# Attention scores: the low part of the queries against the first 1024 keys, in two halves of the array

## The chip, the cores and the metric

The kernel runs on one NeuronCore of a Trainium2 chip. The metric is the device time of one execution in microseconds (us). Three runs of the kernel before gave 2132.44, 2133.23 and 2136.51 us, so the median is 2133.23 us.

## The reference

One layer of a diffusion backbone over 1024 latent tokens of width 1024, with 256 context tokens as a prefix. Only the attention branch matters here: eight heads, each with two softmax maps of width 64, over 1280 keys (1024 latent, 256 context). Cut to what is computed:

```
z = modulate(x, norm1_w, sh1, sc1) @ w_in
q, k = rms_norm(...), rms_norm(...)            # per head and map, width 64, then rotary
s = einsum('bqhmd,bkhmd->bhmqk', q, k_all) * 64 ** -0.5
p = softmax(s, axis=-1)
a = p[:, :, 0] - lam * p[:, :, 1]              # difference of the two maps
o = einsum('bhqk,bkhe->bqhe', a, v_all)
...                                            # S5 branch, gated merge, w_out
x = x + ga1 * merge_branches(...)
x = x + ga2 * conv_ffn(modulate(x, norm2_w, sh2, sc2), w_up, conv_w, conv_b, w_down)
```

All arrays are float32.

## The kernel before

The kernel has three phases. Phase A normalises the tokens, projects them, prepares the S5 branch and spills queries, keys, values and gates to DRAM. Phase B is the attention. Phase C merges the branches and runs the feed-forward part.

Precision: a float32 operand is kept as two float32r parts, a high part and the rest (the low part). `Qd` and `Kd` hold both parts (index `i`). For a head and a map, the tile `K` (L1213) has the high part of the keys on partitions 0 to 63 and the low part on partitions 64 to 127, for 1280 keys. A tile `q` (L1225) holds one part of the queries, and the same 64 rows stand on both halves of the partitions. So one product of 128 rows of a `q` tile with `K` gives that part of the queries times both parts of the keys.

Phase B works on pairs of token tiles, 32 pairs in all (four pairs to a head), in a loop whose order on TensorE, VectorE and ScalarE is written out by hand (`manual_schedule`). In a pair there are four score tiles: two token tiles (`a`, `b`) by two maps, each 128 tokens by 1280 keys in three banks of PSUM (tile `sc`, two of them in flight). `attn_scores` (L1232 to L1241) makes a score tile from six products: for the columns 0 to 512, 512 to 1024 and 1024 to 1280, the high part of the queries (`Q[0]`, L1238) and then the low part (`Q[1]`, L1239). Then VectorE takes the row maximum (L1240), ScalarE the exponentials (L993), VectorE combines the two maps (L1011), TensorE transposes the result (L1020), ScalarE copies the transposes out of PSUM into `at` tiles (L1027, nine buffers), and TensorE multiplies them with the values (L1038). The four score tiles of a pair stand between transposes and value products of the pairs before, so that what follows a score tile on TensorE is a value product (L1038) for two of the four and a transpose (L1020) for the other two.

The loads of phase B are issued by SyncE (SP), whose order a scheduler sets: `K` (L1214), values `V` (L1217), and `q` (L1227 and L1228, eight transfers for half a head). SP issues in order, so a load that waits for a buffer holds back those behind it. Four `K` buffers and four `q` buffers let a head's keys, and half a head's queries, be loaded ahead.

At the start of phase B, TensorE also has four blocks of the S5 branch's last projection to do (`fill`, L1265 to L1267 on tiles `ta` and `tb`), between the first score tiles.

Two other helpers use part of the array and serve the prediction. `ada_part` (L302) multiplies four times with 32 columns of weights, at a place of the array given by `tile_position`. L896 transposes blocks of 32 rows. Both stand between products that use the whole array, such as L417 to L419, L554 to L556 and L891.

Of the kernel before, what the change touches and what calls it, by code (L numbers as in the profile page):

```python
# [10 lines left out]
F32R = mybir.dt.float32r  # L11
# [7 lines left out]
P = 128  # L19
D = 1024          # model width  # L20
KT = D // P       # feature tiles of the model width
L = 1024          # latent tokens
NT = L // P       # token tiles; token n = NT * p + t
NC = 256          # context tokens
LK = L + NC
NKT = LK // P
H = 8             # heads
HD = 64           # width of one map of a head
G = 32            # S5 groups
GC = 16           # channels of a group  # L30
NS = 64           # states of a group
# [7 lines left out]
CH = 8            # tokens per S5 chunk  # L39
NCH = L // CH     # latent chunks  # L40
NCC = NC // CH    # context chunks
FF_PARTS = (5, 5, 4, 4, 4)

# columns of the packed per-partition parameters
# [7 lines left out]
# columns of the constants  # L52
# [4 lines left out]
def pack(x, c, ctx, c_ctx, ada_w, ada_b, norm1_w, w_in, b_gate, q_norm_w, k_norm_w,  # L57
# [3 lines left out]
    """Data layout only: every array sent is a rearrangement of the inputs or depends on shapes alone."""  # L61
    A = {}

    def put(name, a):
        A[name] = np.ascontiguousarray(a)
# [3 lines left out]
    c2 = np.stack([np.asarray(c)[0], np.asarray(c_ctx)], 0)                 # [2, D]  # L69
    put("c2", c2.reshape(2, KT, P).transpose(2, 1, 0))                      # [P, KT, 2]  # L70
    aw = np.asarray(ada_w)[0]
    put("ada0", aw[:, :2048].reshape(KT, P, 2, 4, 256).transpose(3, 1, 0, 2, 4))            # [4, P, KT, 2, 256]
    put("ada", aw[:, 2048:].reshape(KT, P, 2, 4, 512).transpose(2, 0, 1, 3, 4))

    # inside a head map: (row/col, half, i) -> (half, row/col, i)
    def perm64(a):
# [7 lines left out]
    put("win", np.stack([s.reshape(2, 4, P, 512).transpose(0, 2, 1, 3) for s in slabs]))   # [11, 2, P, 4, 512]  # L84
    put("rows", np.concatenate([perm64(np.asarray(q_norm_w)), perm64(np.asarray(k_norm_w)), np.asarray(lam_q1),
                                np.asarray(lam_k1), np.asarray(lam_q2), np.asarray(lam_k2)], 1))  # [1, 384]
# [3 lines left out]

    def st(a):                                                              # [2, G, NS] -> [(d p), G]
        return np.asarray(a).transpose(0, 2, 1).reshape(P, G)

# [15 lines left out]
    def wtiles(a):                                                          # [K, M] -> [M/P, P, K/P, P]  # L109
        k, m = a.shape  # L110
        return a.reshape(k // P, P, m // P, P).transpose(2, 1, 0, 3)
# [8 lines left out]
    # constants of the shapes  # L120
# [3 lines left out]
    n = (NT * np.arange(P)[:, None] + np.arange(NT)[None, :])               # [P, NT]  # L124
# [3 lines left out]
    cs, sn = np.cos(ang), np.sin(ang)                                       # [P, NT, 2, 16]  # L128
# [6 lines left out]
def r32(ap):  # L135
    return ap.bitcast(F32)


class Kern:
# [24 lines left out]
    def pst(self, shape):  # L164
        """One of two banks of PSUM, in turn."""
        self.turn = 1 - self.turn
        return self.t(self.psT, shape, ("ta", "tb")[self.turn], 1)

# [1 line left out]
    def rsqrt_act(self, pool, v, r, tmp):  # L170
        """r = v ** -0.5: seed from the tables, one Newton step."""
# [7 lines left out]
    def rsqrt_dve(self, pool, v, n, tag, bufs=2):  # L179
        """v ** -0.5 on VectorE: seed from the bits, three Newton steps."""  # L180
# [73 lines left out]
    # ---------------------------------------------------------------- phase A  # L254
    def ada_load(self, pool, qt):
        """Weights of shift and scale of the first norm for a quarter of the features."""
# [6 lines left out]
    def ada_first(self, ps, crep, aw):  # L263
        """Two partial sums over the rows of the weights."""
# [27 lines left out]
    def ada_part(self, pool, ps, crep, grp):  # L292
        """Modulation vectors of a group of columns, streamed; yields after each part of the weights."""
# [24 lines left out]
    def phase_a(self):  # L318
# [15 lines left out]
        p0, p0_st = self.pool("p0", "right")  # L334
        TA = 5                                              # token tiles of the first part
# [6 lines left out]
        def pieces(part, k):  # L342
            """Parts of the activations, columns of the input, row of the modulation."""
# [24 lines left out]
        def norm1(acc, late):  # L368
            """Mean square of each token, its -1/2 power on the diagonal of a block, in two parts."""
# [21 lines left out]
        def spread(d):  # L391
            """The scale of each token on all partitions."""
# [8 lines left out]
        def modulate(part, rb, ks):  # L401
            """x s1 rb + shift, as two float32r parts."""
# [197 lines left out]
    def rope_tables(self, zp, kind):  # L600
        """cos and sin times the norm's weights, for queries with the scale of the scores."""
# [18 lines left out]
    def lam(self, zp):  # L620
# [7 lines left out]
        # minus lambda  # L628
# [4 lines left out]
    def qk_post(self, zp, ps, pz, kind, hs, tt):  # L633
        """RMS norm over each head map, rotary, then transposed to [map and width, token]."""
# [68 lines left out]
    def sincos_dve(self, zp, x, n):  # L703
# [20 lines left out]
        # quadrant: k mod 4 = 2 b + o  # L724
# [3 lines left out]
        stt(f, f, -4.0, k, op0=OP.mult, op1=OP.add)             # k mod 4  # L728
# [4 lines left out]
        ts(sb, b, -2.0, 1.0, op0=OP.mult, op1=OP.add)           # sign of the sine  # L733
        ts(cb, o, -2.0, 1.0, op0=OP.mult, op1=OP.add)
        tt(cb, cb, sb, op=OP.mult)                              # sign of the cosine
        ts(d, o, -1.0, 1.0, op0=OP.mult, op1=OP.add)            # 1 - o
# [11 lines left out]
    def cmul(self, eng, o, a, b, tmp):  # L748
        """o = a b on pairs (re, im)."""
# [779 lines left out]
```

## Time and profile before

| | |
|---|---|
| Median of three runs | 2133.23 us (2132.44 to 2136.51) |
| Profiled execution, its span | 2136.6 us |
| TensorE (PE) busy | 2063.8 us, 97% of the span |
| PE weight loads (PEld) busy | 1702.4 us, 80% |
| VectorE (DVE) busy | 1190.6 us, 56% |
| ScalarE (ACT) busy | 743.6 us, 35% |
| GpSimd (POOL) busy | 814.7 us, 38% |
| Phase B, first to last score product | 828.1 to 1202.8 us of the span |

The profiled execution reads like the slowest of the three: its span is within 0.1 us of the highest run and 3.4 us (0.16%) above the median. The ends of matrix products are modelled and overlap, so the busy time of PE is no measure of speed; the distance between the starts of two successive products is what the engine takes for one. A row of PEld is the load of the stationary operand of a product. The granted clock of TensorE is a column of the views by stretch.

### The profile page before, as it was taken

The page shows a single profiled execution, that of the slowest core. Times are in us where ns is not written, and L with a number is a line of the kernel's source. Part 1 is how long each engine was busy: PE and PEld are TensorE (multiplying, and loading weights), DVE is VectorE, ACT ScalarE, POOL GpSimd, SP SyncE. Part 2 cuts the span into 40 slices and gives each one's busy share as a digit, 9 for nine tenths or more (in the row PEclk, how much of TensorE's full clock was granted, in tenths as well). Part 3 has the DMA queues.
Part 4 walks back from the last instruction along what each step waited for, and adds up shares of the span by engine and source line. Part 5 has one row for each costly group of instructions (what it writes and reads, how often), then busy time and mean ns, then how long its engine had stood idle before and what let it go on. Part 6 is the DMA issues. An engine that isn't in the chain of part 4 may idle for free. (4 is left out here: it accounts for less than half of the span.)

```text
span 2136.6 us, 28496 instructions
## 1 busy us (share of the span) xinstructions
PE 2063.8 (97%) x10656; PEld 1702.4 (80%) x10656; DVE 1190.6 (56%) x2363; ACT 743.6 (35%) x1349; POOL 814.7 (38%) x923
## 2 busy tenths in 40 slices
PE   6998999998899999999999989999999999999998
PEld 4777778866577887999999878878888888888887
DVE  6998944799972133888888653443323322233233
ACT  4443424221222312788878601322212212112121
POOL 1476411234311531366666645433323323233221
PEclk9999999999999999999999999999999999999999
DMA  9345565345666327322331145111111111111102
GB/s 323 112 108 139 125 189 176 111 136 165 187 203 220 117 99 227 111 77 77 107 92 53 36 146 185 60 45 50 47 52 50 46 43 45 45 55 43 52 15 99
DMA packets 150506, 227.84 MB, mean 107 GB/s; under 512 B 27104, under 2 KB 85856, under 8 KB 150368
## 3 DMA queue, kind: packets, MB, share of 16 engines
q1 hardware_dynamic: 140288, 207.67, 32.4%
q10 hardware_dynamic: 10080, 18.35, 2.3%
q8 instruction: 84, 1.38, 0.3%
q14 instruction: 54, 0.44, 0.1%
HBM read 168.76 MB, written 57.21 MB: 106 GB/s over the span
## 5 line engine op out<-in xcount | busy, mean ns | idle before, releaser
L1266 PE MATMUL up<-act,whi 128*128 128x512 f32 x704 | 277.3, 394 | 2.4 <-POOL act L1419 2.1
L1265 PE MATMUL up<-act,whi 128*128 128x512 f32 x704 | 275.8, 392 | 0.0
L1267 PE MATMUL up<-act,wlo 128*128 128x512 f32 x704 | 274.5, 390 | 0.0
L1505 DVE SCALAR_TENSOR_TENSOR y<-up,small,y 128x896 f32<-128x896 f32 (+1 forms) x176 | 124.0, 746 | 237.7 <-ACT y L1500 235.9
L1253 POOL TENSOR_TENSOR wlo<-wraw,whi 128x1024 fp32r<-128x1024 f32 (+1 forms) x64 | 141.6, 2212 | 276.0 <-ACT whi L1252 239.0
L1240 DVE TENSOR_REDUCE mx<-sc 128x1 f32<-128x1280 f32 x128 | 190.8, 1491 | 53.9 <-PE sc L1239 53.0
L595 POOL TENSOR_TENSOR wlo<-wraw,whi 128x1024 fp32r<-128x1024 f32 x40 | 97.5, 2453 | 246.9 <-ACT whi L594 246.9
L417 PE MATMUL z<-whi,hTh 128*128 128x512 f32 x448 | 181.6, 409 | 3.6 <-ACT hTh L406 3.6
L418 PE MATMUL z<-wlo,hTh 128*128 128x512 f32 x448 | 180.7, 405 | 0.0
L419 PE MATMUL z<-whi,hTl 128*128 128x512 f32 x448 | 179.3, 402 | 0.2 <-DVE hTl L408 0.2
L993 ACT ACTIVATE e<-sc,mx 128x1280 f32<-128x1280 f32 x128 | 171.9, 1343 | 10.5 <-DVE mx L1240 8.9
L1038 PE MATMUL ta<-V,at 128*128 128x128 f32 x1280 | 168.1, 275 | 0.7 <-ACT at L1027 0.7
L1482 DVE SCALAR_TENSOR_TENSOR x<-z,modT,x 128x512 f32<-128x512 f32 x72 | 53.6, 750 | 203.5 <-PE z L1267 203.5
L1252 ACT CAST whi<-wraw 128x1024 fp32r<-128x1024 f32 (+1 forms) x64 | 61.9, 968 | 294.3 <-PE up L1266 157.0
L1266 PEld LDWEIGHTS up<-act,whi 128*128 128x128 f32 x704 | 132.3, 188 | 31.7 <-POOL act L1419 3.4
L1265 PEld LDWEIGHTS up<-act,whi 128*128 128x128 f32 x704 | 132.2, 188 | 30.6 <-issue 0.2
L1038 PEld LDWEIGHTS ta<-V,at 128*128 128x128 f32 x1280 | 155.4, 191 | 1.0 <-ACT at L1027 0.9
L1267 PEld LDWEIGHTS up<-act,wlo 128*128 128x128 f32 x704 | 132.2, 188 | 28.5
L1238 PE MATMUL sc<-K,q 128*128 128x512 f32 (+1 forms) x384 | 148.6, 387 | 1.6 <-ACT e L993 1.6
L1239 PE MATMUL sc<-K,q 128*128 128x512 f32 (+1 forms) x384 | 131.8, 357 | 0.0
L1253 POOL TENSOR_TENSOR wdlo<-wdraw,wdhi 128x512 fp32r<-128x512 f32 (+1 forms) x40 | 56.3, 1410 | 183.4 <-ACT wdhi L1252 183.2
L1266 PE MATMUL z<-gt,wdhi 128*128 128x512 f32 x320 | 124.6, 389 | 1.0 <-POOL gt L1258 1.0
(436 smaller groups left out, 4662.2 us busy)
## 6 DMA issues: line engine op xcount, KB each, us to landing
wraw<-in_win_dram SPq DMA_DIRECT2D x44, 512.0 KB
wraw<-in_wup_dram SPq DMA_DIRECT2D x44, 512.0 KB
araw<-in_ada_dram SPq DMA_DIRECT2D x32, 512.0 KB
q<-Qd SPq DMA_DIRECT2D x128, 128.0 KB
Kd<-st SPq DMA_DIRECT2D x80, 128.0 KB
K<-Kd SPq DMA_DIRECT2D x16, 640.0 KB
aw<-in_ada_dram SPq DMA_DIRECT2D x16, 512.0 KB
Qd<-st SPq DMA_DIRECT2D x32, 256.0 KB
```

Source lines behind the costliest of these rows:

```text
L417: nc.tensor.matmul(pz, hh, wh, start=k == 0, stop=False)
L418: nc.tensor.matmul(pz, hh, wl, start=False, stop=False)
L419: nc.tensor.matmul(pz, hl, wh, start=False, stop=k == KT - 1)
L993: nc.scalar.activation(em, S[i]["sc"][m][:, :LK], AF.Exp, bias=S[i]["mx"][:, m:m + 1], accum_out=S[i]["l1"] if m else S[i]["l0"])
L1038: nc.tensor.matmul(PO[p][:, j * P:j * P + P], AT[p, kt // 2][:, kt % 2, j * P:j * P + P], W[:, kt], start=kt == 0, stop=kt == NKT - 1)
L1238: nc.tensor.matmul(sc[:, a:b], Q[0][:, m, qs], K[m][:, a:b], start=True, stop=False)
L1239: nc.tensor.matmul(sc[:, a:b], Q[1][:, m, qs], K[m][:, a:b], start=False, stop=True)
L1240: nc.vector.tensor_reduce(S["mx"][:, m:m + 1], sc[:, :LK], axis=AX.X, op=OP.max, negate=True)
L1253: nc.gpsimd.tensor_tensor(l, raw, r32(h), op=OP.subtract)
L1265: mm(o, W[0][:, k], ah[k], start=k == 0, stop=False)
L1266: mm(o, W[0][:, k], al[k], start=False, stop=False)
L1267: mm(o, W[1][:, k], ah[k], start=False, stop=k == n - 1)
```

## The change

The second pass (the low part of the queries) over the keys 0 to 1024 is no longer two products of 128 rows. A new tile `K2` holds the high part of the keys alone: keys 0 to 512 on partitions 0 to 63 and keys 512 to 1024 on partitions 64 to 127. The low part of the queries (which stands on both halves) is multiplied with it in two products of 64 rows and 512 columns, one in the upper half of the array and one in the lower (`tile_position` 0 and 64), each into its own bank of PSUM. The product of the two low parts, which the kernel before adds, is left out for these keys. The columns 1024 to 1280 are made first, in two products of 128 rows as before. `K2` costs two loads of 64 rows for each map and head, and the `at` tiles have seven buffers in place of nine. The diff also takes comments out of the file, and the lines after `attn_load` move down by three to nine.

```diff
         def evac_t(p, c):
             if 0 <= p < NPR:
-                at = self.t(bp, [P, 2, 256], "at", 9)
+                at = self.t(bp, [P, 2, 256], "at", 7)
...
             k = self.t(bp, [P, LK], "K", 4, F32R)
             nc.sync.dma_start(r32(k), self.Kd[h, m].rearrange("i d t -> (i d) t"))
-            K.append(k)
+            k2 = self.t(bp, [P, 512], "K2", 4, F32R)
+            for j in range(2):
+                nc.sync.dma_start(r32(k2[HD * j:HD * j + HD]), self.Kd[h, m, 0, :, 512 * j:512 * j + 512])
+            K.append((k, k2))
...
         sc = self.t(ps, [P, 1536], "sc", 2)
-        for a, b in ((0, 512), (512, 1024), (1024, LK)):
-            nc.tensor.matmul(sc[:, a:b], Q[0][:, m, qs], K[m][:, a:b], start=True, stop=False)
-            nc.tensor.matmul(sc[:, a:b], Q[1][:, m, qs], K[m][:, a:b], start=False, stop=True)
+        k, k2 = K[m]
+        for a, b in ((1024, LK), (0, 512), (512, 1024)):
+            nc.tensor.matmul(sc[:, a:b], Q[0][:, m, qs], k[:, a:b], start=True, stop=False)
+            if a == 1024:
+                nc.tensor.matmul(sc[:, a:b], Q[1][:, m, qs], k[:, a:b], start=False, stop=True)
+        for j in range(2):
+            r = slice(HD * j, HD * j + HD)
+            nc.tensor.matmul(sc[:, 512 * j:512 * j + 512], Q[1][r, m, qs], k2[r], start=False, stop=True,
+                             tile_position=(HD * j, 0))
         nc.vector.tensor_reduce(S["mx"][:, m:m + 1], sc[:, :LK], axis=AX.X, op=OP.max, negate=True)
```

On TensorE, a score tile in the middle of phase B stands like this before, from its third product on (the first two read the same as the third and fourth; `q_9831` is the high part of the queries, `q_9836` the low part, `at` and `V` belong to the value product that follows):

```order
L1238 MATMUL sc_9988<-K_9219,q_9831 128x512
L1239 MATMUL sc_9988<-K_9219,q_9836 128x512
L1238 MATMUL sc_9988<-K_9219,q_9831 128x256
L1239 MATMUL sc_9988<-K_9219,q_9836 128x256
L1038 MATMUL ta_9946<-V_9221,at_9931 128x128 x2
L1020 MATMUL tb_9998<-ident_74,e_2050_9919 128x128
```

The same score tile in the changed kernel, whole, with the value product before and after it (`q_9861` is the high part, `q_9866` the low part, `K_1886_9242` is the new tile; x2 merges two products):

```order
L1038 MATMUL ta_9976<-V_9245,at_9909 128x128 x2
L1242 MATMUL sc_10018<-K_9240,q_9861 128x256
L1244 MATMUL sc_10018<-K_9240,q_9866 128x256
L1242 MATMUL sc_10018<-K_9240,q_9861 128x512 x2
L1247 MATMUL sc_10018<-K_1886_9242,q_9866 128x512 x2
L1038 MATMUL ta_9976<-V_9245,at_9961 128x128 x2
L1020 MATMUL tb_10028<-ident_74,e_2060_9949 128x128
```

There are still six products, but the last two are now those of 64 rows, and they stand between a product of 128 rows and the value product or transpose that follows.

On SP, the loads of the first head stand like this before (`K_7691` and `K_7693` are the two maps):

```order
L1214 DMA K_7691<-Kd 128x1280
L1214 DMA K_7693<-Kd 128x1280
L1217 DMA V_7695<-Vd 128x10x128
L1227 DMA q_7698<-Qd 64x512
L1228 DMA q_7698<-Qd 64x512
```

And like this in the changed kernel (`K_1506_7693` and `K_1508_7698` are the new tiles):

```order
L1214 DMA K_7691<-Kd 128x1280
L1217 DMA K_1506_7693<-Kd 64x512 x2
L1214 DMA K_7696<-Kd 128x1280
L1217 DMA K_1508_7698<-Kd 64x512 x2
L1320 DMA Md<-gate_7528 128x512
L1220 DMA V_7701<-Vd 128x10x128
L1230 DMA q_7704<-Qd 64x512
L1231 DMA q_7704<-Qd 64x512
```

Four loads of 128 KB come in ahead of the values and all eight query loads, and a store `Md` that stood behind the third query load now stands ahead of them too. In the later heads the four loads come in the same way, behind the `K` of their map and ahead of the next half head's queries. The orders of VectorE and ScalarE change in one place each, at the start of phase B, and that of GpSimd nowhere.

## Rows read from the trace of the kernel before

**Rows 1.** Busy time by stretch: start and middle of phase B (us from the span's start).

```profile
core 0: us, PE busy (x) PEld busy (x) DVE busy (x) ACT busy (x) POOL busy (x), PEclk, DMA share, GB/s
828.00:850.00 22.00, 18.52 (x85) 14.52 (x85) 12.44 (x15) 7.47 (x10) 2.68 (x3) 1.00 0.83 270
850.00:1202.00 352.00, 351.24 (x2600) 328.18 (x2599) 296.51 (x388) 286.14 (x572) 209.99 (x506) 1.00 0.28 82
```

**Rows 2.** Waits in 850 to 1202: engine, line, releaser, us in total, times, longest.

```profile
PEld sc L1238 <- ACT e L993: 1.0, 1, 1.0
PE sc L1238 <- ACT e L993: 0.8, 1, 0.8
```

**Rows 3.** PE in order of time, one score tile: start us, us, what.

```profile
1002.87 0.39 PE L1239 MATMUL sc<-K,q 128*128 128x512 f32 x1
1003.10 0.39 PE L1238 MATMUL sc<-K,q 128*128 128x512 f32 x1
1003.33 0.40 PE L1239 MATMUL sc<-K,q 128*128 128x512 f32 x1
1003.57 0.28 PE L1238 MATMUL sc<-K,q 128*128 128x256 f32 x1
1003.68 0.28 PE L1239 MATMUL sc<-K,q 128*128 128x256 f32 x1
1003.80 0.38 PE L1020 MATMUL tb<-ident,e 128*128 128x128 f32 x2
```

**Rows 4.** PEld in order of time, a load in the same score tile.

```profile
1003.11 0.19 PEld L1239 LDWEIGHTS sc<-K,q 128*128 128x128 f32 x1
```

**Rows 5.** The page's costliest groups: the row maxima, one for each score tile.

```profile
L1240 DVE TENSOR_REDUCE mx<-sc 128x1 f32<-128x1280 f32 x128 | 190.8, 1491 | 53.9 <-PE sc L1239 53.0
```

**Rows 6.** PE in order of time, into and out of products of 32 columns.

```profile
662.01 0.39 PE L556 MATMUL z<-hTh,wlo 128*128 128x512 f32 x1
662.33 1.05 PE L302 MATMUL ada<-araw,crep 128*32 128x512 f32 x4
663.31 0.50 PE L554 MATMUL z<-hTh,whi 128*128 128x512 f32 x1
663.65 0.39 PE L555 MATMUL z<-hTl,whi 128*128 128x512 f32 x1
```

**Rows 7.** PEld in the same stretch; in brackets the idle time before.

```profile
662.33 0.14 PEld L302 LDWEIGHTS ada<-araw,crep 128*32 128x32 f32 x4 [0.35 <-issue]
663.31 0.19 PEld L554 LDWEIGHTS z<-hTh,whi 128*128 128x128 f32 x1 [0.84 <-issue]
663.42 0.19 PEld L555 LDWEIGHTS z<-hTl,whi 128*128 128x128 f32 x1
```

**Rows 8.** PE in order of time, into and out of products of 32 rows.

```profile
313.80 0.60 PE L891 MATMUL tb<-ident,u 128*128 128x128 f32 x4
314.33 0.43 PE L896 MATMUL ta<-ident,uc 32*128 32x32 f32 x4
314.69 0.50 PE L418 MATMUL z<-wlo,hTh 128*128 128x512 f32 x1
```

**Rows 9.** Groups by line and shape, PE: busy us, mean ns of one.

```profile
L891 PE MATMUL tb<-ident,u 128*128 128x128 f32 x32 | 4.8, 272 | 0.0
L896 PE MATMUL ta<-ident,uc 32*128 32x32 f32 x32 | 3.4, 227 | 0.0
```

**Rows 10.** Groups by line and shape, PEld: loads of transposes and value products.

```profile
L1038 PEld LDWEIGHTS ta<-V,at 128*128 128x128 f32 x1280 | 155.4, 191 | 1.0 <-ACT at L1027 0.9
L1020 PEld LDWEIGHTS tb<-ident,e 128*128 128x128 f32 x512 | 59.7, 141 | 2.8 <-DVE e L1011 1.8 <-ACT at L1027 0.9
```

**Rows 11.** Busy time by stretch, the loads around the start of phase B.

```profile
814.00:848.00 34.00, 31.91 (x143) 25.63 (x141) 13.20 (x18) 9.40 (x13) 5.15 (x5) 1.00 0.92 294
```

**Rows 12.** SP's queue in order of time: the last query load, then the next half head's first.

```profile
883.44 0.75 SPq L1228 DMA_DIRECT2D q<-Qd  x1
901.57 0.44 SPq L1227 DMA_DIRECT2D q<-Qd  x1
```

## Prediction

> **What bounds the kernel now.** I read the busy time by stretch first. In the 352 us from 850 to 1202, the steady part of the attention, TensorE (PE) is busy for 351.24 us, at a granted clock of 1.00, the level of 2.4 GHz. VectorE is busy for 296.51 us (84%), ScalarE for 286.14 (81%), and the DMA share is 0.28 [rows 1]. Ends of products are modelled, so I looked next at who makes TensorE wait: in the whole stretch the score products wait for ScalarE's exponentials once, for 1.0 us as the load of the weights and 0.8 us as the product [rows 2]. TensorE goes from one product straight to the next, and any time added to or taken from its steps there is time of the kernel, until ScalarE or VectorE, with 55 to 66 us to spare over the stretch, becomes late.
>
> What a step costs is read from the starts of a score tile in order of time. Between 1002.87 and 1003.57 lie three products of 512 columns: 0.233 us each. Those of 256 columns take 0.11 and 0.12 [rows 3]. The load of the weights does not show: the load of the product at 1003.33 begins at 1003.11, under the product before [rows 3, 4]. There are 128 score tiles, one row maximum each [rows 5].
>
> **The change, part by part.** Removed from each score tile: two steps of 512 columns (the low part of the queries over 1024 keys), 0.47 us. Added: two products of 64 rows and 512 columns. If both halves stream at the same time they take one step, 0.233 us. So far that saves 0.233 us a tile.
>
> The part of the array that a product uses is changed by this, once before the pair and once behind it, and the trace of before has places where it changes. At 662.01 a full product starts; the next, of 32 columns, loads its weights at 662.33, 0.32 us later, where an ordinary step is 0.23: 0.09 us more. The load has not been made under the product before, it comes when that one is through [rows 6, 7]. On the way back the same: the load of the full product comes at 663.31 after 0.84 us without one, and the step behind it is 0.34 us (663.31 to 663.65), 0.11 over an ordinary one, which is also the distance of the two loads at 663.31 and 663.42 [rows 6, 7]. With rows in place of columns: four transposes of 128 rows, 0.60 us in all and 272 ns each, so 0.109 apart and the last at 314.13. The first of 32 rows starts at 314.33, 0.20 later, 0.09 over its step. The four take 0.43 us with 227 ns each, so 0.068 apart and the last at 314.53; the full product starts at 314.69, again 0.09 over [rows 8, 9]. So a change of shape costs 0.09 us until the array is through, and then a load that nothing covers.
>
> For 64 rows there is no row. Its drain I take from the 32 rows, 0.09. Its load has 128 columns as a full one: I take 0.11. From below stand the loads of 32 columns, four in 0.14 us [rows 7], so hardly 0.03 each; from above 0.11 for either half in turn. For the way back the next load is that of a value product (191 ns) in two of four score tiles, 0.11 uncovered, and of a transpose (141 ns, so 0.05 less) in the other two [rows 10], 0.06 uncovered: 0.085 on average.
>
> For a tile that is 0.09 + 0.11 + 0.09 + 0.085 - 0.233 = +0.142 us, and for 128 tiles +18.2 us. TensorE had no time to spare, so it is on the path; the row maximum and all behind it come later by as much, and ScalarE and VectorE wait more than before.
>
> The Trainium skill, TensorEngine Tiling (Array Packing), section Theoretical Speedup, gives a contraction of up to 64 rows a factor of up to 2. That would be -0.233 us a tile, -29.8 us in all. The same page, section Key Properties, has the rule that speaks against it, that a change of the tiling mode drains the engine, without a price; the trace agrees with that one.
>
> That the two halves stream together no row of 64 rows shows. The nearest are the four products of 32 columns, which take 1.05 us with all four loads begun within 0.14 us [rows 6, 7]; the two column groups work beside each other there. I take it that halves of rows do too. If not, the pair takes a step more.
>
> Order inside the tile: the 256 columns come first. They take the same two steps, and the loads lie under the products as before. Nothing.
>
> New loads: four for each head, 64 rows by 512 elements of 4 bytes, 131 KB each, 4.2 MB in all. In the middle of the phase the DMA share is 0.28 [rows 1], and SP is free for long: the last query load of a half head is issued at 883.44 and the next half head's first at 901.57, when a half head's buffer comes free [rows 12]. That a half head is loaded ahead leaves 18 us, and four issues of 0.44 to 0.75 us each fit in. If that cover went, a late query load would hold the first score tile of a half head, 16 times. At the start it is different: from 814 to 848 the DMA share is 0.92 at 294 GB/s [rows 11], and TensorE already has 22 - 18.52 = 3.5 us of idle time between 828 and 850 [rows 1]. The tiles of the first head (0.52 MB, 1.8 us at that rate) now go ahead of the values and queries that the first score tile needs, and those of the second follow. From below 0 (the transfers wait behind the fill products), from above 3.6 us for both heads. I take the first head's, 1.8 us.
>
> The `at` tiles, seven for nine: a pair uses five, so a copy takes the buffer of seven copies earlier. For the third to fifth copy of a pair that is the first to third of the pair before, whose last readers stand ahead of the transposes to be copied, on TensorE itself. So it costs nothing; without that order ScalarE would wait for four value products, 0.4 us a pair at 0.11 each, 14 us over 32 pairs.
>
> Sum: 18.2 + 1.8 = +20.0 us. The profiled execution's 2136.6 us become 2156.6. It is 3.4 us over the median of the three runs, 2133.23, and on that median the forecast is 2153 us.
>
> **Rivals.** First, faster: the weights are loaded ahead across the change of shape. A score tile then pays the two drains alone, 0.18 - 0.233 = -0.053 us; over 128 tiles -6.8 us, with the start 2128 us. It decides from the point where more than 0.14 us of a tile's 0.195 us of loads lie under other products. Against it: after 0.35 and 0.84 us without a load, the loads came only when the array was through, and the step behind showed 0.11 [rows 6, 7].
>
> This is what the Trainium skill states for the engine's queue (TensorE: Matmul & The Clock Gate, Part 3, The mechanism): a load that meets no conflict of row groups, or goes to the background buffer, is pulled ahead of products in flight. The rows show that inside one shape [rows 3, 4], not across two.
>
> Second, faster still: the change of shape is free for halves of 64 rows, -29.8 us and the start, 2105 us. ScalarE and VectorE would bear it: the stretch of 352 us would still be over 322, and VectorE is busy for 296.51 of it [rows 1]. Only that no row has 64 rows speaks for it; both shapes that the trace has pay.
>
> Third, slower: the halves stream in turn, because both write all 128 partitions of PSUM. One step more, 0.233 x 128 = 29.8 us: 2183 us. In this case the change doesn't do what it says. For it: the rows show columns beside each other, not rows.
>
> Fourth, slower: the halves stream together, but their loads come one after the other, 0.11 x 128 = 14 us: 2167 us.
>
> **How the numbers follow.** The forecast, drains and uncovered loads with both halves together, has 0.58: 2153 us, by its own bounds 2139 (drains of 0.08 and loads of 0.06 each, no loss at the start) to 2161 (0.10, 0.11 and 3.6 us). Loads in turn 0.09, 2167. Streams in turn 0.14, 2183. Loads ahead 0.08, 2128. Free 0.07, 2105. The remaining 0.04 is a mix of parts that comes out near no change. A measurement of this kernel can tell about 0.2%, 4.3 us, from no change. Faster: 0.07 and 0.06 of the 0.08 at 2128, which is just beyond that, so 0.13. Same: 0.05. Slower: the rest, 0.82. The range goes from 2136 to 2184 us; it leaves out the two faster cases and part of the last.
>
> **What would show it.** In the profile after, L1247 has 256 products, and the two of a pair start within 0.02 us of each other (in turn: 0.23; loads in turn: 0.11). Ahead of their load and of the load behind them PEld shows an idle time with "issue", and the distance from the last 128-row product of a tile to the load is 0.32 us. From the first product of the pair to the next load it is again 0.32. The stretch from 850 to 1202 is longer by 16 to 18 us for the same work, with PE still busy throughout. I am wrong if the loads of the pair begin under the product before, if the step behind them is an ordinary one, or if the attention gets shorter.

## The result and the profile after

Four runs of the changed kernel gave 2144.63 to 2148.33 us, median 2147.53; four of the kernel before 2132.44 to 2136.51, median 2134.47. The ratio is 1.0060, with a 95% interval from 1.0048 to 1.0072: slower by 13.1 us, where the forecast was 20.0 us slower. The profiled execution of the changed kernel has a span of 2145.1 us and took 2146.86. Of the experiments below, one execution of the run on the price of the change of shape took 3254.39 us at a granted clock of 0.593; it is left out of that run's ratio.

Busy time by stretch, the changed kernel (columns as in [rows 1] and [rows 11]):

```profile
814.00:848.00 34.00, 32.24 (x149) 23.51 (x148) 18.04 (x21) 11.72 (x17) 3.81 (x5) 1.00 1.01 297
828.00:850.00 22.00, 21.35 (x104) 15.04 (x103) 14.90 (x18) 11.55 (x18) 1.75 (x3) 1.00 1.02 301
850.00:1202.00 352.00, 352.00 (x2512) 282.00 (x2511) 287.39 (x378) 271.58 (x549) 204.95 (x496) 1.00 0.31 87
```

In the steady part TensorE is as busy as before, 352.00 of 352 us, and at the same granted clock of 1.00, but it finishes 2512 products there where it was 2600 [rows 1]. VectorE and ScalarE have less to do in the same time (287.39 and 271.58 us for 296.51 and 286.14): they wait for TensorE. At the start, 828 to 850, TensorE is busier than before, 21.35 us for 18.52; that was not expected. In part it is the stretch: the first score product starts at 823.7 us here and at 828.3 before.

One score tile and what follows it, TensorE's products in order of time (answers to [rows 3]):

```profile
1002.47 0.37 PE L1242 MATMUL sc<-K,q 128*128 128x256 f32 x1
1002.68 0.28 PE L1244 MATMUL sc<-K,q 128*128 128x256 f32 x1
1002.79 0.62 PE L1242 MATMUL sc<-K,q 128*128 128x512 f32 x2
1003.35 0.50 PE L1247 MATMUL sc<-K,q 64*128 64x512 f32 x2
1003.77 0.66 PE L1020 MATMUL tb<-ident,e 128*128 128x128 f32 x4
1004.26 0.60 PE L1020 MATMUL ta<-ident,e 128*128 128x128 f32 x4
```

Its weight loads; in brackets the idle time of the loading side (answers to [rows 4] and [rows 7]):

```profile
1002.68 0.30 PEld L1242 LDWEIGHTS sc<-K,q 128*128 128x128 f32 x2
1003.34 0.19 PEld L1247 LDWEIGHTS sc<-K,q 64*128 64x128 f32 x2 [0.36 <-issue]
1003.77 0.42 PEld L1020 LDWEIGHTS tb<-ident,e 128*128 128x128 f32 x4 [0.24 <-issue]
1004.16 0.47 PEld L1020 LDWEIGHTS ta<-ident,e 128*128 128x128 f32 x4
```

Two full products begin at 1002.79 and, a step of 0.23 later, at 1003.02; the pair's loads come at 1003.34, 0.32 behind the second. Two loads in 0.19 us, one taking 183 ns, are two loads at the same time. The next load comes 0.42 us behind the pair's. Both idle times end by "issue", that is, by nothing that the profile shows. The four transposes take 0.49 us, from 1003.77 to 1004.26: four steps of 0.109 and 0.05 more. These waits in 850 to 1202 (columns as in [rows 2]):

```profile
PEld sc L1247 <- issue: 42.1, 116, 0.4
PEld ta L1038 <- issue: 14.0, 58, 0.2
PEld tb L1020 <- issue: 13.9, 58, 0.2
```

Every pair pays on both sides: 116 times ahead of the pair, 58 times each ahead of the value product or the transpose behind it. In the kernel before, this list held one wait of 1.0 us [rows 2]. Over the whole run the same is seen in two groups of the page's list, the row maxima (answers to [rows 5]) and the loads of the value products (to [rows 10]; there the idle time was 1.0 us):

```profile
L1249 DVE TENSOR_REDUCE mx<-sc 128x1 f32<-128x1280 f32 x128 | 190.8, 1491 | 63.5 <-PE sc L1247 62.2
...
L1038 PEld LDWEIGHTS ta<-V,at 128*128 128x128 f32 x1280 | 154.9, 191 | 15.7 <-issue 14.5
```

A row maximum and a load take what they took, 1491 and 191 ns; what has grown is the idle time ahead of them, the last figures of each row.

The start of the attention has one wait of the kind that the forecast priced. TensorE's and VectorE's waits in 820 to 850, the changed kernel, each a row of its own view:

```profile
PE sc L1244 <- DMA q<-Qd: 1.1, 1, 1.1
DVE gate L1319 <- DMA gate<-Gd: 8.2, 3, 4.2
```

And the kernel before:

```profile
PE tb L1265 <- DVE gate L1310: 1.3, 1, 1.3
DVE gate L1310 <- DMA gate<-Gd: 7.6, 3, 5.7
```

The low part of the queries is late by 1.1 us, but TensorE's wait for a bank that VectorE holds while it waits for a gate is gone. All of TensorE's waits in this stretch add up to 1.7 us, and to 3.5 in the kernel before.

### The profile page after: what moved, and what is told of

It is laid out like the page before. It is cut to its first block, busy times and chain, and to the rows that moved or that the text cites. A ratio compares the mean times of both kernels' runs of the same rounds, so it can differ in the third digit from the quotient of the medians.

```text
span 2145.1 us, 28539 instructions
## 1 busy us (share of the span) xinstructions
PE 2077.7 (97%) x10656; PEld 1664.2 (78%) x10656; DVE 1191.6 (56%) x2363; ACT 740.7 (35%) x1349; POOL 815.4 (38%) x923
## 5 line engine op out<-in xcount | busy, mean ns | idle before, releaser
L1249 DVE TENSOR_REDUCE mx<-sc 128x1 f32<-128x1280 f32 x128 | 190.8, 1491 | 63.5 <-PE sc L1247 62.2
L1038 PE MATMUL ta<-V,at 128*128 128x128 f32 x1280 | 174.5, 280 | 0.7 <-ACT at L1027 0.7
L1275 PE MATMUL z<-gt,wdhi 128*128 128x512 f32 x320 | 124.6, 389 | 1.0 <-POOL gt L1267 1.0
L1276 PE MATMUL z<-gt,wdlo 128*128 128x512 f32 x320 | 124.3, 389 | 0.0
L1274 PE MATMUL z<-gt,wdhi 128*128 128x512 f32 x320 | 124.0, 390 | 0.0
```

Source lines behind the costliest of these rows:

```text
L1038: nc.tensor.matmul(PO[p][:, j * P:j * P + P], AT[p, kt // 2][:, kt % 2, j * P:j * P + P], W[:, kt], start=kt == 0, stop=kt == NKT - 1)
L1249: nc.vector.tensor_reduce(S["mx"][:, m:m + 1], sc[:, :LK], axis=AX.X, op=OP.max, negate=True)
L1274: mm(o, W[0][:, k], ah[k], start=k == 0, stop=False)
L1275: mm(o, W[0][:, k], al[k], start=False, stop=False)
L1276: mm(o, W[1][:, k], ah[k], start=False, stop=k == n - 1)
```

## The experiments

Each ran beside the kernel before on its chip; ratios are to it, with their 95% intervals. Theory A is the forecast's mechanism.

**The loads alone.** The changed kernel with the second pass in full products; K2 is loaded, and read by nothing.

```diff
             nc.tensor.matmul(sc[:, a:b], Q[0][:, m, qs], k[:, a:b], start=True, stop=False)
-            if a == 1024:
-                nc.tensor.matmul(sc[:, a:b], Q[1][:, m, qs], k[:, a:b], start=False, stop=True)
-        for j in range(2):
-            r = slice(HD * j, HD * j + HD)
-            nc.tensor.matmul(sc[:, 512 * j:512 * j + 512], Q[1][r, m, qs], k2[r], start=False, stop=True,
-                             tile_position=(HD * j, 0))
+            nc.tensor.matmul(sc[:, a:b], Q[1][:, m, qs], k[:, a:b], start=False, stop=True)
```

> The changed kernel with its new loads, its seven at buffers, its order of columns and its order on SP and ScalarE, but the second pass in three products of 128 rows as before (the new tiles are loaded and not read). Theory A (the time comes from the changes of shape of the array, 128 tiles at some 0.12 us): within 3 us of the kernel before, 2131 to 2137 us; in the profile the first score tile may wait up to 2.5 us for a query load as in the changed kernel. Theory B (the loads and orders bring the time): near the changed kernel, 2144 to 2150 us.

Measured: 2131.49 us, ratio 0.9985 (0.9975 to 0.9995). So the loads, the seven `at` buffers and the orders cost nothing here; all that the changed kernel lost stands in the 64-row products, and that is more than its own ratio says: 1.0060 / 0.9985 = 1.0075, or 16 us. One thing differs from the changed kernel: as nothing reads K2, its 24 loads for the last six heads are issued together, between 844 and 867 us of the span, so this run does not try them at their later places. The gain of 3 us is taken up in the runs on the start below.

**Both products in one half.** The second product of a pair goes to the upper half too.

```diff
-            r = slice(HD * j, HD * j + HD)
-            nc.tensor.matmul(sc[:, 512 * j:512 * j + 512], Q[1][r, m, qs], k2[r], start=False, stop=True,
-                             tile_position=(HD * j, 0))
+            r = slice(0, HD)
+            nc.tensor.matmul(sc[:, 512 * j:512 * j + 512], Q[1][r, m, qs], k[r, 512 * j:512 * j + 512],
+                             start=False, stop=True, tile_position=(0, 0))
```

> The changed kernel with both products of 64 rows in the upper half of the array, one after the other, from the high part of the keys in K (the new tiles are loaded and not read). Theory A (the halves stream together and that gives back one step of 0.23 us a tile): 128 x 0.23 = 29.8 us over the changed kernel, 2174 to 2180 us, and in the profile 0.23 us between the starts of the two products of a pair, the changes of shape as before it. Theory C (the halves only look as if they streamed together, since the ends of products are modelled): near the changed kernel, under 2152 us.

Measured: 2178.70 us, ratio 1.0203 (1.0188 to 1.0219), 31 us over the changed kernel. TensorE's products and loads in order of time:

```profile
1002.29 0.73 PE L1247 MATMUL sc<-K,q 64*128 64x512 f32 x2
1002.95 0.66 PE L1020 MATMUL tb<-ident,e 128*128 128x128 f32 x4
```

```profile
1002.29 0.29 PEld L1247 LDWEIGHTS sc<-K,q 64*128 64x128 f32 x2 [0.36 <-issue]
1002.95 0.42 PEld L1020 LDWEIGHTS tb<-ident,e 128*128 128x128 f32 x4 [0.36 <-issue]
```

From the pair to what follows it takes 0.66 us in place of 0.42, a step more. In the changed kernel the two halves do stream together, and the rival of streams in turn falls; that of loads in turn falls by the two loads in 0.19 us above. Over all tiles of 870 to 1200 the second product starts 0.334 us behind the first, where 0.23 was expected. That is no load left uncovered between them: what follows starts 0.324 behind the second, so the two take 0.658 together, and the pair of the changed kernel 0.427, 0.231 less. The second product costs one step and nothing more. Its load begins under the first product: two loads of 0.18 us lie in 0.29, so the second comes 0.11 behind the first. The extra 0.10 is the load of the first product, whose start is recorded with its load (1002.29 in both lists), ahead of its stream.

**The price of the change of shape by itself.** The kernel before, with the last 256-column product of a tile made with 64 rows (the product of the low parts over the 256 context keys is left out). Nothing gets shorter by it.

```diff
-            nc.tensor.matmul(sc[:, a:b], Q[1][:, m, qs], K[m][:, a:b], start=False, stop=True)
+            if a < 1024:
+                nc.tensor.matmul(sc[:, a:b], Q[1][:, m, qs], K[m][:, a:b], start=False, stop=True)
+            else:
+                nc.tensor.matmul(sc[:, a:b], Q[1][0:HD, m, qs], K[m][0:HD, a:b], start=False, stop=True,
+                                 tile_position=(0, 0))
```

> The kernel before, with no new loads, and only the last product of each score tile (low part of the queries, 256 columns) made in 64 rows of the upper half: the same six products with the same columns, so nothing is saved, and the array's shape changes twice a tile (the product of the two low parts is left out for the 256 context keys). Theory A: the bare price of the two changes, 0.09 + 0.11 + 0.09 + 0.08 = 0.37 us a tile, 47 us in all: 2176 to 2184 us, in the profile 0.09 us over a step ahead of the 64-row load and behind it again. Theory D (the price lies in the products of 512 columns or in the two banks, not in the change of shape): under 2150 us.

Measured: ratio 1.0213 (1.0192 to 1.0233), that is 45.5 us, or 0.355 us for each of 128 tiles. The same kernel once more, for its trace:

> One more look at the kernel before with its last 256-column product made with 64 rows (the product of the low parts over the 256 context keys is left out), for a trace at the granted clock of 1.00. Theory A: 2176 to 2184 us; from the first 256-column product to the load of the 64-row product 0.20 us (0.118 for the step and 0.09 until the array is through), from there to the load behind it another 0.20, and the first step behind it 0.06 (transposes) to 0.10 us (value products) over an ordinary one. If the drain were longer for short products than for long ones, the two distances would be over 0.22.

It took 2180.59 us. The products and the loads of one tile's end:

```profile
1004.13 0.28 PE L1238 MATMUL sc<-K,q 128*128 128x256 f32 x1
1004.34 0.38 PE L1242 MATMUL sc<-K,q 64*128 64x256 f32 x1
1004.65 0.66 PE L1020 MATMUL tb<-ident,e 128*128 128x128 f32 x4
```

```profile
1004.33 0.18 PEld L1242 LDWEIGHTS sc<-K,q 64*128 64x128 f32 x1 [0.25 <-issue]
1004.64 0.42 PEld L1020 LDWEIGHTS tb<-ident,e 128*128 128x128 f32 x4
```

The way in is 0.20 us, as expected: 0.118 and 0.09. The way out, from load to load, is 0.31 where I had written 0.20: I had forgotten the product's own load, 0.10, which stands ahead of its stream. From 1004.13 to 1004.65 it is 0.52; less two steps of 0.118 that is 0.28, and with some 0.08 for the load behind 0.36, the price in time. A 256-column product pays no more on the way in than one of 512.

**Two tiles for one change of shape.** The two maps of a token tile are made together: the full products of both, then both pairs.

```diff
+        for m in (1, 0):
+            sc = S["sc"][m] = self.t(ps, [P, 1536], "sc", 2)
+            for a, b in ((1024, LK), (0, 512), (512, 1024)):
...
+        for m in (1, 0):
+            sc = S["sc"][m]
+            for j in range(2):
...
+            nc.vector.tensor_reduce(S["mx"][:, m:m + 1], sc[:, :LK], axis=AX.X, op=OP.max, negate=True)
```

> The changed kernel with the two maps of a token tile made together: full products of both score tiles, then the four products of 64 rows, then the two row maxima, so that the shape changes once for two tiles. Theory A: a tile pair costs TensorE 2 x 0.233 less for the saved steps and once 0.37 more, -0.09 us, so with TensorE as the bound 64 x -0.09 = -6 us against the kernel before, 2125 to 2132 us. Rival E (the two score buffers are taken and freed together, and TensorE waits for the exponentials): in the profile L1239 waits for ScalarE in most pairs, and the time is above the kernel before, 2140 us or more, whatever the changes of shape cost.

Measured: 2205.59 us, ratio 1.0330 (1.0316 to 1.0344). TensorE is busy for only 304.42 of the 352 us from 850 to 1202, and waits:

```profile
PE tb L1020 <- ACT at L1027: 23.0, 50, 0.7
PE tb L1081 <- ACT at L1027: 21.0, 22, 1.0
PE ta L1038 <- ACT at L1027: 2.7, 3, 0.9
```

The rival of this run wins, in another form than written. The score products hardly wait; the transposes do, for a bank that ScalarE has yet to empty. And ScalarE waits in the same stretch:

```profile
ACT e L993 <- DVE mx L1248: 53.6, 26, 2.3
```

Its copies stand in its queue behind exponentials whose row maxima, behind both pairs, come later than before. What a second pair costs TensorE can be read from the loads all the same:

```profile
1002.77 0.30 PEld L1246 LDWEIGHTS sc<-K,q 64*128 64x128 f32 x4 [0.36 <-issue]
1003.43 0.52 PEld L1038 LDWEIGHTS ta<-V,at 128*128 128x128 f32 x4 [0.36 <-issue]
```

The loads of both pairs lie in 0.30 us, and the next load comes 0.66 us behind the first, where it is 0.42 behind a single pair: one step more, and no load.

**The same, mirrored, with its control.** The first map has its pair last and the second its pair first, so that the first map's row maximum is not late; the control makes the second pass in full products in the same order. `ctx` makes the two products of 256 columns, `pair` the two that are of 64 rows or, in the control, full.

```diff
...
+            if m:
+                ctx()
+            else:
+                pair(True)
+            for a, b in cols[1:]:
+                mm(sc[:, a:b], hi, k[:, a:b], start=m == 1, stop=m == 0)
+            if m:
+                pair(False)
+            else:
+                ctx()
...
```

> From the changed kernel: the two maps of a token tile are made one behind the other, the first with its pair of 64-row products last and the second with its pair first, so that two pairs stand together and one change of shape into 64 rows and one out of it serve two score tiles (64 of each in place of 128). What stands between the score tiles of a pair of token tiles is moved so that the two gaps have six groups of products each. By theory A (a change in and out costs 0.12 + 0.233 = 0.353 us, and a pair streams in one step) two score tiles cost 0.353 - 0.466 = -0.113 us against full products in the same order, 64 times: 7.2 us less than the run of the same order with full products, so 2124 to 2126 where TensorE never waits. Theory E (score buffers are taken two at a time, and TensorE waits for exponentials): up to 70 us longer as in the run with both pairs at the end, with idle time of TensorE that ends by ScalarE; then the difference to the control is less than 7 us or none.

> The control of the run with mirrored tiles: the same order of tiles and products, the K2 loads too, but the second pass of the queries over the first 1024 keys in full products of 128 rows. Where TensorE never waits it has the same work as the run with the loads alone, 2131 to 2133 us; by theory E it is longer, by 5 to 60 us, with idle time of TensorE that ends by ScalarE. By theory A the mirrored run is 7.2 us below this one.

Measured: 2203.73 us, ratio 1.0318 (1.0302 to 1.0333), and 2207.71 us, 1.0336 (1.0321 to 1.0352). TensorE's waits from 850 to 1240, mirrored and then control:

```profile
PE tb L1020 <- ACT at L1027: 26.9, 57, 1.1
PE ta L1038 <- ACT at L1027: 18.9, 28, 0.7
```

```profile
PE tb L1020 <- ACT at L1027: 25.7, 56, 0.7
PE ta L1038 <- ACT at L1027: 19.6, 29, 0.7
```

Both wait for ScalarE's copies, so the order alone costs some 70 us, and the intervals of the two overlap: in time it stays unclear whether the mirrored pairs gain. The trace says more. Between 870 and 1200 two tiles take 2.382 us from the first product to what follows and 2.442 in the control, 0.06 less where I expected 0.113. In half of these, 24 of 48 and 23 of 47, nothing holds up the score products: 2.345 us against 2.424, 0.079 less. There the second pair's load begins 0.108 us behind the first's, and the next product starts 0.66 us behind the first pair, one step over a single pair, as in the two runs above. In the other half that load begins 0.306 us behind the first's, and 0.040 is left of the gain; in the control the load of the second tile's first product comes as late in every second pair of tiles, and its releaser is ScalarE's exponential. The terms of the table below give 0.466 - 0.094 - 0.19 - 0.10 = 0.08, with 0.10 for the load of the full product that stands behind the pairs here. On a TensorE that never waits, two pairs side by side would so gain 0.08 us for two tiles, 5 us in all; that is an estimate from these steps, and no run's time shows it.

**The start: the first exponential ahead of a cast.** In the changed kernel ScalarE makes the attention's first exponential ahead of the third of the last casts of weights, where it waited 7.5 us for their transfer before. The kernel before with that alone:

```diff
                 exps(a, 1)
+                if q == 0:
+                    self.late()
...
-        for m in range(KT - NL + 1, KT):
-            prep(m)
+        self.late = lambda: prep(KT - 1)
```

> The kernel before with one thing moved: the last block of weights of the S5 branch (its load, its cast on ScalarE and its two gates) is asked for after the first exponentials of the attention, so that ScalarE makes the first exponential ahead of the third of the last three casts, as it does in the changed kernel. The orders of TensorE, VectorE, GpSimd and SyncE stay. No K2, no products of 64 rows. Theory S (the start of the attention gained in the changed kernel because this cast, which waits for a late transfer, no longer holds up the first exponentials): 2 to 3 us shorter than the kernel before, about 2133, ratio 0.9985 to 0.999, the whole gain of the run with the loads alone; the idle time of 7.5 us of ScalarE with the wraw transfer as its releaser is gone or stands behind an exponential, and from the first to the last score product the trace is about 2 us shorter than the 411.7 us of before. Rival T (the gain came from the columns' order in the score tile, from seven `at` buffers or from where the loads stand on SP): no change, ratio 0.9995 to 1.0005.

Measured: 2135.76 us, ratio 1.0001 (0.9992 to 1.0009). Theory S falls. The trace shows why; TensorE, and below it by stretch (PEclk, the granted clock, is the third column from the end):

```profile
837.37 0.50 PE L1267 MATMUL tb<-h5h,whi 128*128 128x512 f32 x1 [2.29 <-DVE gate L1312]
839.54 0.63 PE L1268 MATMUL tb<-h5l,whi 128*128 128x512 f32 x1
839.97 0.63 PE L1269 MATMUL tb<-h5h,wlo 128*128 128x512 f32 x1
```

```profile
836.00:838.00 2.00, 0.63 (x3) 0.54 (x4) 1.37 (x2) 0.00 (x0) 0.00 (x0) 1.00 0.88 256
840.00:842.00 2.00, 2.00 (x6) 1.61 (x5) 1.84 (x4) 0.34 (x3) 0.00 (x0) 0.51 0.88 308
```

TensorE is 0.99 us ahead at the 24th product of the attention, but waits 0.8 us for a gate soon after it, and at the 36th it is level with the kernel before. At the next gate it stands still for 2.29 us, where that was 1.3. Behind this wait and some five steps at the granted clock of 1.00 the clock is at 0.51 in this execution (the level of 1.2 GHz), and seven steps take 0.43 us in place of 0.23, 1.4 us more.

**The start: the gates ahead.** On SP, K2 had moved more than the loads beside it: in the trace four loads of `gate` are issued ahead of the keys of the second head's second map, where it was one (three more, where the expectation below has two). The kernel before with the second head asked for one pair later, alone and together with the edit above:

```diff
-                if q % 4 == 1 and q // 4 + 1 < H:
+                if (q == 2 or q % 4 == 1 and q > 1) and q // 4 + 1 < H:
                     head(q // 4 + 1)
```

> The kernel before, with the second head's keys and values asked for one pair of token tiles later. On SP the four loads of `gate` for the blocks that fill the start of the attention then stand ahead of the second head's keys (and so do the second half of the first head's queries), as two of them do in the changed kernel; in the kernel before and in the run with the first exponential ahead they stand behind those keys. ScalarE's order is that of before. Theory G (the start gained in the changed kernel and in the run with the loads alone because these gates came earlier, so that the fill products did not wait for a bank that VectorE holds while it waits for a gate): 1.5 to 3.5 us faster, ratio 0.9985 to 0.9993, VectorE's idle time with the gate transfer as its releaser 5.7 us shorter at its longest, the wait of TensorE for VectorE at the gates gone. Rival T (the columns' order or seven `at` buffers): no change, 0.9995 to 1.0005.

> The run with the gates ahead, and the first exponential ahead of the last cast too. Theory G with the cast as a second wait behind it: the first exponential ahead of the cast gave 1.0 us by the 24th product of the attention and lost it to a gate; with both, 2.5 to 4.5 us faster than before, ratio 0.998 to 0.9988, as much as the run with the loads alone or more. Rival T: no change.

Measured: 2131.24 us, ratio 0.9985 (0.9977 to 0.9994), and 2130.51, 0.9985 (0.9976 to 0.9995). VectorE's wait for the gates in 820 to 850, with the gates ahead (first) and with both:

```profile
DVE gate L1310 <- DMA gate<-Gd: 2.3, 3, 1.6
```

```profile
DVE gate L1312 <- DMA gate<-Gd: 1.3, 1, 1.3
```

Theory G holds: one line on the order of loads gives 3 us, without K2, and TensorE no longer waits for VectorE at a gate. The edit moves the second half of the first head's queries ahead too; what that is worth by itself is not shown. Nor is it the same 3 us as in the run with the loads alone: by the 200th product that one is only 0.7 us ahead, with its late queries, and the gates give 3.4. The second edit adds nothing in time that these runs can tell. These versions beat both kernels of this case.

## Why the prediction was right, and where it was off

The likeliest case came true, with its mechanism: a change of shape costs more than the step that it saves. The terms against the trace, as means over the starts of all products of whole score tiles between 870 and 1200 (115 tiles before, 109 after):

| Term, us a tile | Forecast | Measured |
|---|---|---|
| Drain ahead of the pair | 0.09 | 0.094 (0.327 - 0.233) |
| The pair's load and the drain behind it | 0.20 | 0.19 (0.423 - 0.233) |
| Uncovered load behind | 0.085 | 0.080 (0.102 and 0.057 by halves) |
| Step saved | -0.233 | -0.233 |
| Order inside the tile | 0 | -0.012 |
| Sum | +0.142 | +0.119 |

*What it removes.* Right: the products of a pair start 0.003 us apart. What no row of 64 rows showed before was taken from products of 32 columns [rows 6, 7], and it carried over. The Trainium skill's factor of up to 2 (TensorEngine Tiling (Array Packing), section Theoretical Speedup) is there in the streaming of the pair, two products in one step; the tile became longer all the same.

*What it adds.* Right to 0.011 us, 0.364 for 0.375. The drain from 32 rows and columns, 0.09, and the load of a full product, 0.11, stood in for those of 64 rows and came out at 0.094 and about 0.10. One sign does not fit the prediction's own terms: it wanted 0.32 us from the first product of the pair to the next load, where they give 0.11 + 0.233 + 0.09 = 0.43; 0.42 was measured. The first rival, loads ahead, did not come true across the change of shape: on both sides the load comes behind an idle time, 0.36 and 0.24 us. The rule of the Trainium skill that this rival weighed (TensorE: Matmul & The Clock Gate, Part 3, The mechanism) holds in these runs inside one shape alone: between full products, between the two halves of a pair, whose loads begin together, and between two 64-row products in the same half, where the second load begins 0.11 us behind the first.

*Order inside the tile.* Put at nothing, it gives back a little. The run with the loads alone shows it without the pairs: 1.252 us a tile for 1.264. It is a few ns in each of several steps, and I have no cause for it. Three other traces with the order of before have 1.260, so that up to 0.004 of it is no more than what two traces differ by. On 128 tiles it is 1 to 1.5 us.

*The sum on the path.* 0.119 x 128 = 15.2 us against 18.2. TensorE had no time to spare, and every bit of it arrived: from the first score product to the 3000th product behind it the trace of after is 13.2 us longer, as the time is. From the 200th on, where the start is over, 14.2 us are added in 116 tiles, 0.122 each.

*The start of the attention.* This is the step that was wrong: "the tiles of the first head now go ahead of the values and queries that the first score tile needs", +1.8 us. The loss is there, as a wait of 1.1 us for the queries, and 1.3 in the run with the loads alone. But I priced only the loads that stand beside K2 on SP and not those further down that changed places with the second head's: three gates came ahead of the keys of its second map. The time from the first score product to the n-th product behind it, worked out from the starts in each trace:

| n | before | after | loads alone | exponential first | gates ahead | both |
|---|---|---|---|---|---|---|
| 12 | 2.35 | 3.90 | 3.92 | 2.35 | 2.35 | 2.35 |
| 24 | 6.10 | 6.77 | 6.69 | 5.11 | 5.11 | 5.11 |
| 60 | 15.58 | 14.94 | 14.50 | 18.04 | 12.95 | 12.94 |
| 200 | 39.34 | 38.30 | 38.65 | 40.61 | 35.93 | 35.52 |

At 12 the changed kernel is 1.55 us behind, by the late queries and its first two tiles; at 60 it is 0.64 ahead. The edit for the gates alone gives 3.4 us by 200. So the term is some -2 us, not +1.8: 13.1 measured less 15.2 for the tiles. Both errors, 3 us of the tiles and 4 of the start, lie on the same side. The pairs themselves cost 16 us, the distance to the run with the loads alone, which has the same loads at the start.

*Seven `at` buffers and the later loads.* Right: no loss in the run with the loads alone, which speaks for the buffers; for the later loads speaks that between 850 and 1202 the changed kernel's products wait for nothing but the changes of shape.

## What to carry to other kernels

Packing the array by halves pays only if the pairs between two changes of shape save more than these cost: here some 0.36 us for going in and out, against 0.233 us for each step saved. A single pair between full products loses 0.13 us; a second pair right behind it pays one step and no load, so that two tiles gain 0.08 us. The orders that brought two pairs together here cost 70 us in other waits, so the gain is worth having only where the order allows it. A trace that has any change of shape, even of another shape, gives the price: look for the load that comes late with "issue" as its releaser, and measure from load to load, as the first product behind a change is recorded with its load and not with its stream. When an edit adds loads, compare the whole order of the queue behind them, not only the neighbours: what else changed places may be worth as much.

## What the runs showed of the hardware

- A load of 64 rows of weights takes as long as one of 128 (183 ns for 190). It does not begin under a full product (0.36 us of idle time ahead of it), but it does under a 64-row product, even in the same half: 0.11 us behind that one's load, and two such products take one step of 0.23 us more than one. Loads into the two halves run at the same time, two in 0.19 us.
- Behind a wait of 2.29 us at the start of the attention the granted clock was at its lower level for some 3 us, which cost 1.4 us in one execution. The kernel before has such a stretch too, near its own start, which the changed kernel's profile has not; busy time by stretch, before and then after:

```profile
26.00:30.00 4.00, 3.84 (x19) 2.25 (x16) 0.45 (x1) 1.32 (x2) 1.39 (x1) 0.50 1.02 405
```

```profile
26.00:30.00 4.00, 3.63 (x17) 2.68 (x18) 1.74 (x6) 1.32 (x2) 2.38 (x1) 1.00 1.01 396
```

- The first score product starts at 828.3 us of the span in one profile and at 823.7 in the other, with the same work ahead of it (822.3 to 829.3 over eleven profiles here). That stretch does not explain it: the run with the first exponential ahead has one as well (granted clock 0.57 from 26 to 30) and starts at 823.6, that with the gates ahead has none and starts at 825.2. A comparison of two spans is no better than that; distances inside the attention are, and they gave 13.2 us for the 13.1 measured. In the other runs the distance to the 3000th product comes within 1.7 us of the measured time.
